# Feature-major weight tiles at all 64 pairs of eight start offsets

## The chip, the cores and the metric

The kernel runs on one core of a Trainium2 chip. The metric is the device time of one execution in microseconds. Engines are named as the profile does: PE is TensorE's matmuls, PEld its weight loads, DVE is VectorE, ACT is ScalarE, POOL is GpSimd, SP is SyncE, which issues most DMAs.

## The reference, cut to what matters

One encoder layer for 256 tokens of width 2048, all in float32. Nearly all of the arithmetic is seven dense products of an activation matrix with a weight matrix that is read once from HBM:

```python
proj = h @ w_in                              # 2048 x 18464, split into the heads of two mixers
x = x + merged @ w_out                       # 2048 x 2048
q = h @ w_q; k, v = split(mem_n @ w_kv)      # 2048 x 2048, 2048 x 4096
x = x + o @ w_o                              # 2048 x 2048
x = x + square(relu(h @ w_ff1)) @ w_ff2      # 2048 x 8192, 8192 x 2048
```

Between them lie norms, retention, a gated delta rule, and a cross-attention with four heads.

## The kernel before, in words

**Split operands.** Each float32 operand of a product is kept as a high part (`hi`, rounded to the type float32r by an ACT copy) and a low part (`lo`, the remainder, by a DVE subtraction). A product is then high x high + high x low + low x high. Activations stand in `Quad` tiles named `q`: four 128-row blocks of features, each with 256 high and 256 low columns beside each other.

**Weights.** `fetch` (L75) loads 1 MB of weights into a tile `raw` of [128, 2048] with one DMA on SP's queue, and splits it in two halves of 1024 columns: ACT writes `whi` (L93), DVE writes `wlo` (L94). Both names are rings of four buffers of 1024 + ROOM = 1088 columns, that is 4352 bytes in each partition, and ROOM lets the 1024 columns in use start a little after the buffer's start. `raw` is a ring of three. The fetches have the highest priority, so that they run ahead of the products as far as the rings allow.

**Two kinds of calls.** `chunk` (L120) is token-major: a block of activations is the stationary operand of TensorE, 512 columns of weights are the moving operand, and three matmuls (L134 to L136) make a product. `blocks` (L158) is feature-major: a block of 128 weight columns is stationary and the activations move. With `nb = 2`, which all calls use, one call takes 256 weight columns over all 16 blocks of 128 rows. For each such block (a *step* here) it does two matmuls with a high weight block against 512 columns (the activation's high and low parts at once, L172), and then two with a low weight block against 256 columns (the high part, L174). A call has 16 steps, 64 matmuls and two fetches, or four pairs of `whi` and `wlo`. There are 96 such calls in the program: for the attention's keys, queries and output, for the parts of the mixers that are wanted feature by feature, for the output projection, and for the first MLP matrix.

A third kind, `seven_products` (L1014), does part of the second MLP matrix with weight tiles `sh` and `sl` as moving operands of 256 columns.

**Where the tiles lie.** In the built program each `whi`, `wlo` and `q` buffer starts 224 bytes after a multiple of 256 in its partition. `chunk` uses offset 0 in the weight buffers, so that stationary and moving operands start equally far after a multiple of 256. `blocks` passes `at=SHIFT`, 48 elements or 192 bytes, for both parts. So its weights start 160 bytes after a multiple of 256, against 224 for the activations. `seven_products` shifts `sh` and `sl` by the same SHIFT; there the stationary operand is at 224 and the moving one at 160. All blocks within a tile are multiples of 512 bytes apart, so that these distances hold for every matmul of a call.

The instruction order is made at build time by a scheduler; semaphores follow from the tiles.

Of the kernel before, what the change touches and what calls it, by code (L numbers as in the profile page):

```python
# [11 lines left out]
F32R = mybir.dt.float32r  # L12
# [5 lines left out]
P = 128  # L18
# [15 lines left out]
SHIFT, ROOM = 48, 64  # L34
# [16 lines left out]
def trunk(ctx: ExitStack, tc: tile.TileContext, x, mem, positions, norm_mix_g, w_in, conv_w, gdn_a_log, gdn_dt_bias,  # L51
# [8 lines left out]
    wp = ctx.enter_context(tc.tile_pool(name="wpipe", bufs=3))  # L60
# [5 lines left out]
    def stream_ps():  # L66
        s0 = psp.tile([P, 512], F32, name="s0", tag="s0", bufs=2)
        s1 = psp.tile([P, 512], F32, name="s1", tag="s1", bufs=2)
        return s0, s1
# [2 lines left out]
        return psp.tile([P, 512], F32, name="b", tag="b", bufs=4)  # L72


    def fetch(pieces, k, n, rush=False, hold=None, at=0):  # L75

        raw = wp.tile([P, k * n], F32, name="raw", tag="raw", bufs=3)
        rv = raw.rearrange("p (k n) -> p k n", k=k)
        with tc.high_priority(offset=100000):
            for off, ap in pieces:  # L80
                src = ap.rearrange("(k p) n -> p k n", p=P)
                for ks in ((slice(0, k // 2), slice(k // 2, k)) if rush else (slice(0, k),)):
                    nc.sync.dma_start(rv[:, ks, off:off + ap.shape[1]], src[:, ks, :])
            got = []
            for i in range(2):
                if hold:
                    both = hold().both
                    hi, lo = (both[:, a:a + 2, :].rearrange("p a s -> p (a s)") for a in (0, 2))
                else:
                    hi, lo = (wp.tile([P, 1024 + ROOM], F32R, name=e, tag=e, bufs=4)[:, at:at + k * n // 2]  # L90
                              for e in ("whi", "wlo"))
                src = raw[:, i * k * n // 2:(i + 1) * k * n // 2]
                act.activation(hi, src, AF.Copy)  # L93
                vec.tensor_sub(lo, src, hi.bitcast(F32))  # L94
                got.append((hi.rearrange("p (k n) -> p k n", n=n), lo.rearrange("p (k n) -> p k n", n=n)))
        return got
# [23 lines left out]
    def chunk(quads, pieces_of, evac, before=None, hold=None, between=None):  # L120
# [4 lines left out]
        if hold:  # L125
            parts[1:] = [(1, 0, 256, ps[1][:, :256]), (1, 256, 512, bank()[:, :256])]
        held = {q: fetch(pieces_of(q), 4, 512, hold=hold) for q in ((2, 3) if hold else ())}

        def products(q, i, part, halves):
# [8 lines left out]
        for q in range(4):  # L138
            if q not in held:
                if before:  # L140
                    before(q)
                halves = fetch(pieces_of(q), 4, 512, rush=before is not None and q == 0)
                for i in range(4):
                    for part in parts:
                        products(q, i, part, halves)
                    if between and i % 2:
                        between()
# [10 lines left out]
    def blocks(quads, w, c0, nb, evac, whole=None, ahead=50000):  # L158

        k = 16 // nb
        ps = stream_ps()
        n = nb * P
        for g in range(KT // k):
            halves = fetch([(0, w[g * k * P:(g + 1) * k * P, c0:c0 + n])], k, n, at=SHIFT)
            for i in range(k):
                kk = g * k + i
                xh, xhl = quads[kk // 4][0][:, kk % 4, :], quads[kk // 4].both[:, kk % 4, :]
                wh, wl = (a[:, i % (k // 2), :] for a in halves[i // (k // 2)])  # L170
                for b in range(nb):
                    pe.matmul(ps[b], wh[:, b * P:(b + 1) * P], xhl, start=kk == 0, stop=False)  # L172
                for b in range(nb):
                    pe.matmul(ps[b][:, :S], wl[:, b * P:(b + 1) * P], xh, start=False, stop=kk == KT - 1)  # L174
        if whole:
            with tc.high_priority(offset=50000):
                o = whole()
                for b in range(nb):
                    act.activation(o[:, b, :], ps[b][:, S:], AF.Copy)
                    vec.tensor_add(o[:, b, :], o[:, b, :], ps[b][:, :S])  # L180
                evac(o)
            return
        for b in range(nb):
            with tc.high_priority(offset=ahead):
                o = sm.tile([P, S], F32, name="bo", tag="bo", bufs=2)
                act.activation(o, ps[b][:, S:], AF.Copy)  # L186
                vec.tensor_add(o, o, ps[b][:, :S])  # L187
                evac(b, o)
# [146 lines left out]
    for k2 in range(8):  # L335
# [10 lines left out]
        for f in range(2):  # L346
            k = 2 * k2 + f
# [171 lines left out]
    for b2 in range(8):  # L519
        ko = kv.tile([P, 2, S], F32, name="ko", tag="vo", bufs=2)  # L520

        def evac_k(b, ps):
            vec.tensor_mul(ko[:, b, :], ps, mrow)

        blocks(memq, w_xkv[0], b2 * 256, 2, evac_k)
        nc.sync.dma_start(kt_d[:, 2 * b2:2 * b2 + 2, :], ko)
        for h in ((0,), (2, 4), (6, 8), (10,), (12,), (14,), (), ())[b2]:
            decays(h)
        if 2 <= b2 < 6:
            ret_decays(2 * b2 - 4)  # L530
# [20 lines left out]
    for q in range(4):  # L551
        at = slice(32 * q, 32 * q + 32)
# [6 lines left out]
    def gdn_stream(grp):  # L559
# [4 lines left out]
        for pr in range(2):  # L564
# [5 lines left out]
            for part, c0, bofs in ((1, C_GQ, 0), (0, C_GK, 16), (2, C_GV, 32)):  # L570
                def evac(b, ps, part=part, bofs=bofs):
                    if part < 2:
                        conv_silu(bofs + h0 + b, ps, kq[:, b, part, :])
                    else:
                        vt = mx.tile([P, S], F32, name="vt", tag="vt", bufs=2)
                        conv_silu(bofs + h0 + b, ps, vt)
                        vts.append(vt)
                blocks(h1, w_in[0], c0 + h0 * GD, 2, evac)
# [171 lines left out]
    def retention(j, yr):  # L750
        qk = mx.tile([P, 4, S], F32, name="qk", tag="qk", bufs=1)

        for a2, c0 in ((0, C_RQ), (2, C_RK)):
            def evac_qk(b, ps):

                rb = mx.tile([P, S], F32, name="rb", tag="rb", bufs=2)
                act.activation(rb[0:64], ps[64:128], AF.Copy)
                act.activation(rb[64:128], ps[0:64], AF.Copy)
                o = qk[:, a2 + b, :]
                vec.tensor_mul(o, ps, cos)  # L760
                vec.tensor_mul(rb, rb, sin)
                vec.tensor_add(o, o, rb)

            blocks(h1, w_in[0], c0 + 256 * j, 2, evac_qk)
# [169 lines left out]
    for h in range(XH):  # L934
# [32 lines left out]
        for d2 in range(2):  # L967
            ops = bank()
            ov = ops.rearrange("p (d s) -> p d s", d=2)
            for d in range(2):  # L970
                c0 = (2 * d2 + d) * P
# [94 lines left out]
    for fb in range(4):  # L1066
# [6 lines left out]
        for b2 in range(8):  # L1073
# [3 lines left out]
            at = slice(b2 % 2 * 2, b2 % 2 * 2 + 2)  # L1077
# [15 lines left out]
        for n in range(1, 4):  # L1093
# [13 lines left out]
            def evac_last(t, ps, c0, c1):  # L1107
# [20 lines left out]
                for c in (0, 3, 1, 2):  # L1128
# [17 lines left out]
                  hold=quad_b if last else None)  # L1146
# [37 lines left out]
```

## Time and profile before

| | |
|---|---|
| time, median of 2 runs | 2065.16 us (2065.08 to 2065.25) |
| profiled execution | 2066.05 us, its span 2064.3 us |
| PE busy | 2045.1 us, 99% of the span |
| DVE busy | 1510.3 us, 73% |
| ACT busy | 1132.2 us, 55% |
| granted TensorE clock | 0.999 |
| HBM traffic | 197 GB/s over the span |

The span runs from the first to the last instruction; 1.75 us of the profiled execution lie outside it. A matmul's listed duration includes its passage through the array, in which the next one has already begun. The pace of matmuls is therefore read from the start of one to the start of the next, not from durations.

### The profile page before, as it was taken

Reading aid. Unit: us, or ns where it says so; the run is one execution under the profiler, and the core shown is the slowest. Engines: PE = TensorE matmul, PEld = TensorE weight load, DVE = VectorE, ACT = ScalarE, POOL = GpSimd, SP = SyncE. Lnnn points to the kernel's source line nnn. Section 1 sums busy time; section 2 is a strip of 40 time slices with the busy share of each in tenths; the row PEclk is TensorE's granted clock in tenths of the full one; section 3 lists DMA queues with packets and bytes.
Section 4 is the critical chain, followed back from the end, with each engine's and each line's share of the span. In section 5 each row is a group of like instructions: output and inputs, shape, how many; then the busy total and the mean of one; then the engine's idle time right before and its main releaser. Section 6 shows DMA issues by size and latency. Waiting matters only on the chain.

```text
span 2064.3 us, 29089 instructions
## 1 busy us (share of the span) xinstructions
PE 2045.1 (99%) x11240; PEld 1774.0 (86%) x11240; DVE 1510.3 (73%) x2381; ACT 1132.2 (55%) x1669; POOL 26.9 (1%) x37
## 2 busy tenths in 40 slices
PE   8999999999999999999999999999999999999998
PEld 6888888888888888888888898888888888988887
DVE  6785888588957896688767665768758756775885
ACT  7564664556445644565456555555546545554664
POOL 0000000000000000000000000000000000000000
PEclk9999999999999999999999999999999999999999
DMA  8797655465556555655567664565656566656653
GB/s 302 229 313 233 207 192 199 164 208 181 198 183 199 183 195 189 189 182 180 189 192 234 194 193 147 182 189 181 224 184 198 179 204 194 194 194 195 192 198 129
DMA packets 328313, 408.28 MB, mean 198 GB/s; under 512 B 31200, under 2 KB 236528, under 8 KB 328048
## 3 DMA queue, kind: packets, MB, share of 16 engines
q1 hardware_dynamic: 328032, 405.92, 61.0%
q8 instruction: 88, 1.44, 0.3%
q10 hardware_dynamic: 144, 0.52, 0.1%
q14 instruction: 49, 0.40, 0.1%
HBM read 391.19 MB, written 15.22 MB: 197 GB/s over the span
## 4 chain that ended last, share of the span: by engine, by line
PE 97%; DMA 1%; SPq 1%; issue 0%; DVE 0%; ACT 0%; POOLq 0%; POOL 0%; DVEq 0%; ACTq 0%
PE s L172 34%; PE s L174 17%; PE s L135 12%; PE s L134 12%; PE s L136 12%; PE b L1041 1%; PE b L1042 1%; PE b L1043 1%; PE b L689 1%; DMA xc<-x 1%; PE b L590 1%; PE b L104 0%; PE b L105 0%; PE b L106 0%; SPq L290 0%
## 5 line engine op out<-in xcount | busy, mean ns | idle before, releaser
L94 DVE TENSOR_TENSOR wlo<-raw,whi 128x1024 fp32r<-128x1024 f32 x668 | 816.0, 1223 | 412.6 <-ACT whi L93 405.7
L93 ACT ACTIVATE whi<-raw 128x1024 fp32r<-128x1024 f32 x668 | 706.6, 1060 | 689.1 <-PE s L172 331.2
L172 PE MATMUL s<-q,whi 128*128 128x512 f32 x3072 | 959.7, 392 | 2.2 <-DVE bo L187 2.1
L174 PEld LDWEIGHTS s<-q,wlo 128*128 128x128 f32 x3072 | 575.3, 188 | 123.6
L174 PE MATMUL s<-q,wlo 128*128 128x256 f32 x3072 | 611.9, 280 | 0.0
L172 PEld LDWEIGHTS s<-q,whi 128*128 128x128 f32 x3072 | 468.8, 188 | 5.2 <-DVE bo L187 2.5
L134 PE MATMUL s<-whi,q 128*128 128x512 f32 x1136 | 443.6, 392 | 0.7 <-ACT whi L93 0.7
L135 PE MATMUL s<-wlo,q 128*128 128x512 f32 x1136 | 443.5, 390 | 0.6 <-DVE wlo L94 0.6
L136 PE MATMUL s<-whi,q 128*128 128x512 f32 x1136 | 441.8, 390 | 0.0
L135 PEld LDWEIGHTS s<-wlo,q 128*128 128x128 f32 x1136 | 213.9, 188 | 43.5 <-DVE wlo L94 1.1
L134 PEld LDWEIGHTS s<-whi,q 128*128 128x128 f32 x1136 | 213.7, 188 | 42.9 <-ACT whi L93 1.1
L136 PEld LDWEIGHTS s<-whi,q 128*128 128x128 f32 x1136 | 213.3, 188 | 42.8 <-DVE q L257 0.2
L541 DVE SCALAR_TENSOR_TENSOR acc<-bo,cw,acc 128x255 f32<-128x255 f32 (+1 forms) x144 | 61.3, 479 | 3.3 <-ACT acc L538 3.0
L1029 ACT ACTIVATE sh<-raw 128x768 fp32r<-128x768 f32 x32 | 27.1, 847 | 49.1 <-DMA raw<-w_ff 32.5
L187 DVE TENSOR_TENSOR bo<-bo,s 128x256 f32<-128x256 f32 x128 | 47.9, 415 | 0.0
L649 DVE TENSOR_TENSOR pr<-lw,tw 32x31 f32<-32x31 f32 (+15 forms) x124 | 40.2, 324 | 8.7 <-DMA lw<-scr_l 7.1
L651 DVE TENSOR_TENSOR tw<-tw,pr 32x31 f32<-32x31 f32 (+15 forms) x124 | 40.5, 327 | 2.2
L186 ACT ACTIVATE bo<-s 128x256 f32<-128x256 f32 x128 | 41.0, 370 | 0.0
L1030 DVE TENSOR_TENSOR sl<-tt,sh 128x1024 fp32r<-128x1024 f32 x32 | 39.1, 1223 | 0.0
L1029 ACT ACTIVATE sh<-tt 128x1024 fp32r<-128x1024 f32 x32 | 33.6, 1051 | 8.4 <-DVE tt L1023 8.4
L1043 PE MATMUL b<-sh,cm 128*128 128x256 f32 x128 | 35.5, 279 | 0.0
L1042 PE MATMUL b<-sl,cm 128*128 128x256 f32 x128 | 35.5, 279 | 0.0
(359 smaller groups left out, 1575.5 us busy)
## 6 DMA issues: line engine op xcount, KB each, us to landing
raw<-w_in SPq DMA_DIRECT2D x143, 1024.0 KB, 5.1
raw<-w_ff SPq DMA_DIRECT2D x128, 1024.0 KB, 5.8
raw<-w_xkv SPq DMA_DIRECT2D x31, 1024.0 KB, 6.4
raw<-w_out SPq DMA_DIRECT2D x16, 1024.0 KB, 5.9
raw<-w_xq SPq DMA_DIRECT2D x16, 1024.0 KB, 5.4
raw<-w_xo SPq DMA_DIRECT2D x16, 1024.0 KB, 5.4
dec_d<-dec_w SPq DMA_DIRECT2D x8, 384.0 KB, 7.9
dec<-dec_d SPq DMA_DIRECT2D x8, 384.0 KB, 4.2
```

The costliest lines, as they stand in the source:

```text
L93: act.activation(hi, src, AF.Copy)
L94: vec.tensor_sub(lo, src, hi.bitcast(F32))
L134: pe.matmul(o, xh, wh, start=first, stop=False)
L135: pe.matmul(o, xh, wl, start=False, stop=False)
L136: pe.matmul(o, xl, wh, start=False, stop=last)
L172: pe.matmul(ps[b], wh[:, b * P:(b + 1) * P], xhl, start=kk == 0, stop=False)
L174: pe.matmul(ps[b][:, :S], wl[:, b * P:(b + 1) * P], xh, start=False, stop=kk == KT - 1)
L187: vec.tensor_add(o, o, ps[b][:, :S])
L541: vec.scalar_tensor_tensor(acc[:, d:], ps[:, :S - d], cw[:, j, blk:blk + 1], acc[:, d:], op0=ALU.mult, op1=ALU.add)
L1029: act.activation(sh[:, xs, :], src, AF.Copy)
L1042: pe.matmul(o, lhs[0], sl[:, x, :], start=False, stop=False)
L1043: pe.matmul(o, lhs[1], sh[:, x, :], start=False, stop=last and i == 1 and (m % 2 == 1 or m == 6))
```

## The change

The single offset of `fetch` becomes a pair, one for the high and one for the low tiles. Each call of `blocks` takes a running number `u` and uses the offsets 8 (u mod 8) for the high parts and 8 (u // 8 mod 8) for the low parts, in elements: 0, 8, ..., 56, or 0 to 224 bytes in steps of 32. After 64 calls the pairs start again; the 96 calls use every pair, and those with a low offset of 0, 8, 16 or 24 twice. `chunk` keeps offset 0, `seven_products` its SHIFT.

```diff
+    placed = []
+
-    def fetch(pieces, k, n, rush=False, hold=None, at=0):
+    def fetch(pieces, k, n, rush=False, hold=None, at=(0, 0)):
...
-                    hi, lo = (wp.tile([P, 1024 + ROOM], F32R, name=e, tag=e, bufs=4)[:, at:at + k * n // 2]
-                              for e in ("whi", "wlo"))
+                    hi, lo = (wp.tile([P, 1024 + ROOM], F32R, name=e, tag=e, bufs=4)[:, a:a + k * n // 2]
+                              for e, a in zip(("whi", "wlo"), at))
...
         k = 16 // nb
+        u = len(placed)
+        placed.append(u)
         ps = stream_ps()
         n = nb * P
         for g in range(KT // k):
-            halves = fetch([(0, w[g * k * P:(g + 1) * k * P, c0:c0 + n])], k, n, at=SHIFT)
+            halves = fetch([(0, w[g * k * P:(g + 1) * k * P, c0:c0 + n])], k, n, at=(8 * (u % 8), 8 * (u // 8 % 8)))
```

In the built programs the order of instructions on every engine, their waits' places, the buffers' addresses and the shapes are the same before and after. What differs is the start address within the buffer of what L93 and L94 write and what the weight loads of L172 and L174 read.

## The prediction

> **What bounds the kernel now.** First the page's busy times, its clock row and the chain that ended last.
>
> ```profile
> PE 2045.1 (99%) x11240; PEld 1774.0 (86%) x11240; DVE 1510.3 (73%) x2381; ACT 1132.2 (55%) x1669; POOL 26.9 (1%) x37
> PEclk9999999999999999999999999999999999999999
> PE 97%; DMA 1%; SPq 1%; issue 0%; DVE 0%; ACT 0%; POOLq 0%; POOL 0%; DVEq 0%; ACTq 0%
> PE s L172 34%; PE s L174 17%; PE s L135 12%; PE s L134 12%; PE s L136 12%; PE b L1041 1%; PE b L1042 1%; PE b L1043 1%; PE b L689 1%; DMA xc<-x 1%; PE b L590 1%; PE b L104 0%; PE b L105 0%; PE b L106 0%; SPq L290 0%
> ```
>
> TensorE makes 97% of the chain, at full granted clock. The two matmul lines of the feature-major calls alone, L172 and L174, are 34% and 17% of 2064.3 us, about 1053 us. Does TensorE ever wait for the tiles that the change moves? The table of its waits, whole, and the groups of the two lines that write those tiles answer it.
>
> ```profile
> PE b L246 <- DMA xc<-mem: 4.8, 1, 4.8
> PE b L232 <- DMA grow<-norm_mem_g: 2.5, 1, 2.5
> PE s L172 <- DVE bo L187: 2.1, 2, 1.1
> PE s L134 <- ACT whi L93: 0.7, 1, 0.7
> PE s L135 <- DVE wlo L94: 0.6, 1, 0.6
> L94 DVE TENSOR_TENSOR wlo<-raw,whi 128x1024 fp32r<-128x1024 f32 x668 | 816.0, 1223 | 412.6 <-ACT whi L93 405.7
> L93 ACT ACTIVATE whi<-raw 128x1024 fp32r<-128x1024 f32 x668 | 706.6, 1060 | 689.1 <-PE s L172 331.2
> ```
>
> TensorE waited 10.7 us in all, and 1.3 us of it for `whi` and `wlo`, both times in a token-major call. The other way round, ACT stood idle 331.2 us before L93 because the matmuls of L172 still held a buffer. The weights are ready early. So the time of a feature-major call is the pace of its matmuls, and that pace is read from starts in the timeline. Here is the end of a token-major call and the start of a feature-major one ("x2" merges two matmuls; columns are start, us, engine, line, output and inputs), and then where the same call ends.
>
> ```profile
> 1534.14 0.39 PE L134 MATMUL s<-whi,q 128*128 128x512 f32 x1
> 1534.37 0.39 PE L135 MATMUL s<-wlo,q 128*128 128x512 f32 x1
> 1534.60 0.39 PE L136 MATMUL s<-whi,q 128*128 128x512 f32 x1
> 1534.82 0.62 PE L172 MATMUL s<-q,whi 128*128 128x512 f32 x2
> 1535.28 0.39 PE L174 MATMUL s<-q,wlo 128*128 128x256 f32 x2
> 1535.51 0.62 PE L172 MATMUL s<-q,whi 128*128 128x512 f32 x2
> ...
> 1545.17 0.62 PE L172 MATMUL s<-q,whi 128*128 128x512 f32 x2
> 1545.62 0.40 PE L174 MATMUL s<-q,wlo 128*128 128x256 f32 x2
> 1545.86 0.62 PE L172 MATMUL s<-q,whi 128*128 128x512 f32 x2
> ```
>
> The call begins at 1534.82 and the next one at 1545.86: 11.04 us for 16 steps, **0.690 us a step**. 96 calls of 16 steps are 1536 steps (3072 matmuls of L172, two a step), and 1536 x 0.690 = 1060 us, which agrees with the chain's 1053. The token-major triple takes 1534.82 - 1534.14 = 0.68, or 226.7 ns for 512 columns.
>
> **The change part by part.** Nothing is added, removed or moved in order: the same instructions, shapes, DMAs and buffers, in the same places of every queue. Three things could still change.
>
> *The writes.* L93 and L94 write at offsets of 0 to 56 elements. The trace has two of the offsets, 0 in token-major calls and 48 in feature-major ones, mixed in one group:
>
> ```profile
> L94 DVE TENSOR_TENSOR wlo<-raw,whi x668: 1149/1226/1245, 6.1 to 2036.1; 128x1024 fp32r<-128x1024 f32 x167
> L93 ACT ACTIVATE whi<-raw x668: 1039/1061/1096, 5.0 to 2034.0; 128x1024 fp32r<-128x1024 f32 x167
> ```
>
> All 668 lie between 1149 and 1245 ns and between 1039 and 1096 ns (least, median, most), so these two offsets cost at most some per cent. I put the writes at nothing. The cover is the idle time above: L93 would have to become 689.1 / 668, about 1 us, longer each time before ACT had no idle time left ahead of it; DVE has 554 us of idle time in the span, 0.8 us for each L94.
>
> *The matmul pace as a function of the offset.* This is the whole question. A weight load and a matmul read at the same time, so their places in memory may matter:
>
> ```profile
> 1535.40 0.30 PEld L172 LDWEIGHTS s<-q,whi 128*128 128x128 f32 x2
> 1535.74 0.42 PEld L174 LDWEIGHTS s<-q,wlo 128*128 128x128 f32 x2
> ```
>
> The load at 1535.74, of 0.19 us, is the one of L174 and begins 0.23 us after the matmul at 1535.51, just as that line's second matmul begins: the load for the next matmul runs beside the current one. The Trainium skill, page "TensorE: Matmul & The Clock Gate", section "Step-by-step: what each phase is for", says that TensorE has two independent read ports and that such a load takes no read bandwidth from the running matmul. By that rule the offsets are free and the sum of this change is zero. The rows do not settle this, because 256-column matmuls are seen at more than one pace. Here is `seven_products` twice, first its slower and then its faster pace, and a stretch of a token-major call with 256 columns.
>
> ```profile
> 1416.58 0.28 PE L1041 MATMUL b<-sh,q 128*128 128x256 f32 x1
> ...
> 1419.06 0.63 PE L172 MATMUL s<-q,whi 128*128 128x512 f32 x2
> 1421.18 0.62 PE L172 MATMUL s<-q,whi 128*128 128x512 f32 x2
> ...
> 1424.65 0.28 PE L1042 MATMUL b<-sl,q 128*128 128x256 f32 x1
> 1426.58 0.39 PE L172 MATMUL s<-q,whi 128*128 128x512 f32 x1
> ...
> 2036.13 0.40 PE L134 MATMUL s<-whi,q 128*128 128x512 f32 x1
> 2036.83 0.28 PE L134 MATMUL s<-whi,q 128*128 128x256 f32 x1
> 2037.54 0.40 PE L134 MATMUL s<-whi,q 128*128 128x512 f32 x1
> ```
>
> From 1416.58 to 1419.06 stand 21 matmuls: 118.1 ns each. From 1424.65 to 1426.58 stand 17: 113.5 ns. Six from 2036.83 to 2037.54: 118.3 ns. The feature-major call that begins at 1419.06 does its first three steps by 1421.18 at **0.707 us**, against the usual 0.690. So the pace depends on something besides the columns, and the same offsets show two paces: a phase between loads and matmuls that a call enters with, besides the place. The three distances between stationary and moving start that the kernel has (0 in token-major calls; 64 bytes one way in feature-major calls and the other way in `seven_products`) all lie between 113.5 and 118.3 ns for 256 columns. With distance 0, a feature-major step put together from token-major rows would be 2 x 226.7 + 2 x 118.3 = 690.0 ns in the usual phase, the same as now, and 2 x 233.3 + 2 x 118.3 = 703 ns in the slow one (2036.13 to 2036.83 is 0.70 for three).
>
> So of the eight offsets, 0, 16 and 48 elements have a row near them and show no cost of their own in the usual phase. The other five (8, 24, 32, 40, 56) have no row. Both bounds for such a step: at best every matmul goes at the fastest paces seen, 2 x 226.7 + 2 x 113.5 = 680 ns, which is 10 ns less; at worst it goes at 707 ns, which is 17 ns more. Over all 1536 steps that is **-15 us to +26 us**. I take, for these offsets, the slow pace in one step of three, since the usual pace is what all three distances with a row show most of the time and is the nearest. About 0.6 of the operands fall on the five offsets (5 of 8 for the high parts, 56 of 96 calls for the low parts): 1536 x 0.6 x 17 ns / 3 = 5 us.
>
> *The lead of the weights.* A longer call would give ACT and DVE more time, a shorter one less. At the lower bound they still have the idle time above, so no wait comes late.
>
> **Sum.** Against the profiled execution: 2066.05 + 5 = 2071. The median before is 0.9 us below that execution, so **2070 us**.
>
> **The rivals.**
>
> 1. *Offsets don't matter* (and the two paces are phase alone). For it: all three distances with rows give the same 690 ns. Against it: nothing but the paces' spread. Time: 2065.
>
> 2. *Some pairs are better.* If the five offsets stall less often, the faster pace of 113.5 becomes usual. Time at the bound: 2065 - 15 = 2050. To be faster by over 2% (41.3 us, which is also about what this measurement can tell from no change), each of the 6144 matmuls would have to lose 6.7 ns on average, more than the 118.1 - 113.5 = 4.6 ns between the paces seen. That needs a pace that no row shows.
>
> 3. *Offsets at odd multiples of 32 bytes are dear: slower.* Every tile that TensorE now reads in these products starts at a multiple of 64 bytes from every other (224 and 160 after a multiple of 256). The change puts half of the high tiles and half of the low ones, 3072 matmuls, on starts that are 32 bytes off that raster. If the two reads hinder each other there and a load runs partly behind its neighbour, each such matmul is longer by a part of the load's 0.19 us. An eighth of it, 24 ns, gives 3072 x 24 = 74 us and 2139; the whole of it would be 584 us. The rival decides from 41.3 us / 3072 = 13.4 ns per affected matmul. For it: no row excludes it. Against it: the dearest matmul in the rows above takes 233 ns for 512 columns, some 7 ns over the usual.
>
> 4. *The change does not do what it says*: were the pairs not all used, or the buffers moved, the sum would differ. The built program has the 64 pairs and unmoved buffers, so this gets no chance of its own.
>
> **How the numbers follow.** Forecast (slightly slower, 2066 to 2092): 0.50. Rival 1 (2064 to 2066): 0.20. Rival 2 within its bound (2048 to 2064): 0.16, and beyond 2%: 0.03. Rival 3 over 2%: 0.11. The range reaches from rival 2's bound to the worst of the slow pace with a little of rival 3, **2048 to 2096**, and leaves out about 0.14. Faster by over 2%: 0.03; within 2%: 0.86; slower: 0.11.
>
> **What would show it.** The page should keep PE at 99% with the same counts, and the waits of TensorE for `whi` and `wlo` should stay near 1.3 us: that tests the writes and the lead. The 96 calls, read from start to start, should mostly take between 10.9 and 11.4 us (16 steps at 680 to 707 ns), with the call's length a function of its pair that repeats after 64 calls; the token-major triple should stay at 0.68 us. If calls of all pairs take 11.04, rival 1 is right. If calls with an odd u stand out by over half a microsecond, rival 3 is. The prediction is wrong if any pairs run far outside 680 to 707 ns a step, since all of it rests on paces that were seen at three distances only.

## The result, and the profile after

| | before | after |
|---|---|---|
| time, median of 2 runs | 2065.16 us | 2079.64 us (2079.45 to 2079.84) |
| ratio | | 1.007, 95% interval 1.0054 to 1.0087 |
| profiled execution / its span | 2066.05 / 2064.3 us | 2079.45 / 2077.7 us |

The change makes the kernel 14.5 us slower. That lies within the range, on the side that was forecast, but is three times the rise in the sum. In the changed kernel L93, L94, L172 and L174 have become L95, L96, L176 and L178, and the token-major L134 to L136 have become L136 to L138. The page's busy times, clock, chain, and the groups that matter:

```profile
PE 2060.4 (99%) x11240; PEld 1779.9 (86%) x11240; DVE 1509.8 (73%) x2381; ACT 1132.3 (54%) x1669; POOL 26.9 (1%) x37
PEclk9999999999999999999999999999999999999999
PE 98%; DMA 1%; issue 0%; ACT 0%; DVE 0%; SPq 0%; POOLq 0%; POOL 0%; ACTq 0%
L96 DVE TENSOR_TENSOR wlo<-raw,whi 128x1024 fp32r<-128x1024 f32 x668 | 815.4, 1222 | 425.7 <-ACT whi L95 422.6
L95 ACT ACTIVATE whi<-raw 128x1024 fp32r<-128x1024 f32 x668 | 706.9, 1060 | 701.0 <-PE s L176 351.0
```

The counts are the same and the granted clock is 0.999 in both. The writes take what they took (1222 and 1060 ns against 1223 and 1060). ACT waits even longer for the matmuls to give a buffer back, 351.0 us against 331.2. All waits of TensorE's matmuls:

```profile
PE b L250 <- DMA xc<-mem: 4.7, 1, 4.7
PE b L236 <- DMA grow<-norm_mem_g: 2.6, 1, 2.6
PE s L176 <- DVE bo L191: 1.5, 2, 1.1
```

None is for `whi` or `wlo`. (One weight load of L137 still waits 0.5 us for `wlo`.) Taking the time from each matmul's start to the next and adding it up by line, the two feature-major lines grew by 10.0 us (L172, now L176) and 4.4 us (L174, now L178); no other line changed by more than 0.6 us. So the whole loss is in the pace of the feature-major matmuls. The timeline shows it from call to call, each beginning at one of these rows (calls with the pairs (48, 56) and (56, 56) in elements, then after "..." the one with (16, 0), and the call after it):

```profile
1343.00 0.62 PE L176 MATMUL s<-q,whi 128*128 128x512 f32 x2
1354.39 0.62 PE L176 MATMUL s<-q,whi 128*128 128x512 f32 x2
1365.48 0.63 PE L176 MATMUL s<-q,whi 128*128 128x512 f32 x2
...
1392.20 0.63 PE L176 MATMUL s<-q,whi 128*128 128x512 f32 x2
1403.61 0.62 PE L176 MATMUL s<-q,whi 128*128 128x512 f32 x2
```

11.39, 11.09 and 11.41 us. In each kernel, 47 of the 96 calls run through without other work on TensorE between their steps: before, each of them took 11.04 us, and now they take 11.09 to 11.41. Below is the mean step in ns of every pair, worked out from the starts in the trace, over all steps that no other work breaks into; the instruction order, which is the built program's, tells which call has which pair. Each entry rests on one or two calls. Eight steps of 776 to 811 ns are left out: the same steps of the same calls last 774 to 807 ns in the kernel before, so their length is not the offsets' doing.

```
high \ low   0      8     16     24     32     40     48     56   elements
 0         696.7  703.4  699.4  699.2  699.9  699.9  694.7  700.4
 8         700.8  702.7  697.4  702.8  701.7  704.1  700.7  702.7
16         712.2  700.0  694.3  699.4  700.1  713.5  694.4  698.7
24         700.0  700.1  700.7  703.7  703.5  700.1  705.4  694.6
32         706.9  699.8  705.4  700.4  699.7  700.1  703.1  699.3
40         702.6  704.4  709.2  700.1  708.3  700.0  699.3  699.6
48         699.9  700.3  703.2  694.3  703.3  706.8  690.1  712.4
56         693.7  699.3  704.3  694.2  696.7  700.1  697.3  693.1
```

The best is (48, 48), the pair of the kernel before; the next, (56, 56), is at 693.1. The mean of all these steps is 700.9 ns against 690.7 before; 10.2 ns x 1536 steps = 15.7 us, which is the loss but for what the other lines give back and the steps left out. Most calls settle within a few steps and then repeat a short pattern of steps (their *pace*) until other work breaks in or they end. In the kernel before, the pattern is 687 and 693 ns in turn.

### The profile page after: what moved, and what is told of

It is laid out like the page before. It is cut to its first block, busy times and chain, and to the rows that moved or that the text cites. A ratio compares the mean times of both kernels' runs of the same rounds, so it can differ in the third digit from the quotient of the medians.

```text
span 2077.7 us, 29089 instructions
## 1 busy us (share of the span) xinstructions
PE 2060.4 (99%) x11240; PEld 1779.9 (86%) x11240; DVE 1509.8 (73%) x2381; ACT 1132.3 (54%) x1669; POOL 26.9 (1%) x37
## 4 chain that ended last, share of the span: by engine, by line
PE 98%; DMA 1%; issue 0%; ACT 0%; DVE 0%; SPq 0%; POOLq 0%; POOL 0%; ACTq 0%
PE s L176 34%; PE s L178 17%; PE s L136 13%; PE s L137 13%; PE s L138 12%; PE b L1045 1%; PE b L1047 1%; PE b L1046 1%; PE b L693 1%; PE b L594 1%; PE b L106 0%; PE b L107 0%; PE b L108 0%; DMA vr<-vv_d 0%; DMA xc<-mem 0%
## 5 line engine op out<-in xcount | busy, mean ns | idle before, releaser
L96 DVE TENSOR_TENSOR wlo<-raw,whi 128x1024 fp32r<-128x1024 f32 x668 | 815.4, 1222 | 425.7 <-ACT whi L95 422.6
L95 ACT ACTIVATE whi<-raw 128x1024 fp32r<-128x1024 f32 x668 | 706.9, 1060 | 701.0 <-PE s L176 351.0
L176 PE MATMUL s<-q,whi 128*128 128x512 f32 x3072 | 968.3, 395 | 1.6 <-DVE bo L191 1.5
L178 PEld LDWEIGHTS s<-q,wlo 128*128 128x128 f32 x3072 | 574.9, 188 | 132.7
L178 PE MATMUL s<-q,wlo 128*128 128x256 f32 x3072 | 615.9, 281 | 0.0
L176 PEld LDWEIGHTS s<-q,whi 128*128 128x128 f32 x3072 | 472.7, 188 | 4.7 <-DVE bo L191 2.0
L137 PE MATMUL s<-wlo,q 128*128 128x512 f32 x1136 | 443.4, 390 | 0.0
L136 PE MATMUL s<-whi,q 128*128 128x512 f32 x1136 | 443.2, 392 | 0.0
L138 PE MATMUL s<-whi,q 128*128 128x512 f32 x1136 | 441.8, 390 | 0.0
L137 PEld LDWEIGHTS s<-wlo,q 128*128 128x128 f32 x1136 | 213.9, 188 | 43.0 <-DVE wlo L96 0.5
L138 PEld LDWEIGHTS s<-whi,q 128*128 128x128 f32 x1136 | 213.5, 188 | 43.0
L136 PEld LDWEIGHTS s<-whi,q 128*128 128x128 f32 x1136 | 213.8, 188 | 42.2 <-ACT q L260 0.4
L1033 ACT ACTIVATE sh<-tt 128x1024 fp32r<-128x1024 f32 x32 | 33.7, 1052 | 10.2 <-DVE tt L1027 10.2
L1025 DVE TENSOR_TENSOR tt<-raw 128x1024 f32<-128x1024 f32 x16 | 19.6, 1224 | 22.5 <-DMA raw<-w_ff 22.5
```

Source lines behind the costliest of these rows:

```text
L136: pe.matmul(o, xh, wh, start=first, stop=False)
L137: pe.matmul(o, xh, wl, start=False, stop=False)
L138: pe.matmul(o, xl, wh, start=False, stop=last)
L1033: act.activation(sh[:, xs, :], src, AF.Copy)
```

## The experiments

**Does the place set the pace, or the change of place from call to call?** By the first idea (theory 1, the place theory) each pair has its own pace; by the second (theory 2) only the change costs. In the first two runs all 96 calls have one pair: one of the dearest, (16, 0), and then (0, 0).

```diff
-... k, n, at=(8 * (u % 8), 8 * (u // 8 % 8)))
+... k, n, at=(16, 0))        # and in the second run: at=(0, 0)
```

> All 96 feature-major calls with the one pair (16, 0), which in the swept kernel had steps of 713 ns in both of its calls. If the place sets the pace (theory 1): 713 - 690 = 23 ns a step over 1536 steps, 35 us over the kernel before, about 2100. If it is the change of offsets from call to call that costs (theory 2): one pair only, so about 2065.

Measured: 2096.48 us, 1.0151 of the kernel before (1.0136 to 1.0166), or 31 us over it where theory 1 expected 35. Two calls in a row in the timeline, beginning at

```profile
1403.73 0.63 PE L176 MATMUL s<-q,whi 128*128 128x512 f32 x2
1415.14 0.64 PE L176 MATMUL s<-q,whi 128*128 128x512 f32 x2
```

are 11.41 us apart, 713 ns a step, and the median step of every one of the 96 calls is 713. The place sets the pace; the change from call to call is not needed for it.

Could it be where ACT and DVE write the tiles, and not where TensorE reads them? In the 47 calls of this run without other work, 7 steps have no write to `whi` or `wlo` beside them. They average 713.3 ns, the other 745 steps 713.1. So the slow pace does not come from a write under way.

> All feature-major calls with the pair (0, 0). Theory 1: 697 ns a step as in the swept kernel, 7 x 1536 = 11 us over before, about 2076. Theory 2: 2065. My prediction's step put together from token-major rows (690 ns at distance 0): 2065 as well.

Measured: 2073.82 us, 1.0041 (1.0026 to 1.0055), or 9 us over before where theory 1 expected 11 and theory 2 nothing.

```profile
146.08 0.63 PE L176 MATMUL s<-q,whi 128*128 128x512 f32 x2
157.22 0.63 PE L176 MATMUL s<-q,whi 128*128 128x512 f32 x2
```

11.14 us, 696 ns a step, as for this pair in the swept kernel (696.7 in the table). So distance 0, at which the prediction had put a step together from token-major rows to 690 ns, is not free in a feature-major call.

**Is it the distance between the operands, or the absolute address?** The kernel before with all tiles 32 bytes lower, and then the kernel before with only the feature-major weights 256 bytes further (the rings get the room for it; `sh` and `sl` keep their size and their offset).

```diff
-    cp.tile([P, 56], F32, name="pad0")
+    cp.tile([P, 48], F32, name="pad0")
```

> The kernel before with every tile moved down by 32 bytes, all distances kept. If only the distance between the two operands counts: 2065, with 0.690 us a step. If the raster of absolute addresses counts (rival 3 in another form): a step changes by several ns in feature-major and token-major calls, several us at least.

```diff
-SHIFT, ROOM = 48, 64
+SHIFT, ROOM = 48, 128
...
-... k, n, at=SHIFT)
+... k, n, at=(SHIFT + 64, SHIFT + 64))
```

> The kernel before with the feature-major offset 64 elements (256 bytes) further, 112 for both parts, and rings that have room for it. If only the distance within 256 bytes counts: 0.690 us a step and 2065. If the full distance counts: another pace, as between pairs of the sweep, 5 to 35 us over.

Measured: 2064.78 us, ratio 0.9998 (0.9988 to 1.0007), and 2065.95 us, ratio 1.0004 (0.9995 to 1.0013). Both are the time of before. Neither a common shift by 32 bytes nor 256 bytes more between the operands moves the pace; the mean step of both runs is within 0.1 ns of before. So far as these two shifts of one pair can show it, what counts is the distance of the operands within 256 bytes, not the address.

**One part alone.**

```diff
-... at=(8 * (u % 8), 8 * (u // 8 % 8)))
+... at=(8 * (u % 8), SHIFT))        # and in the second run: at=(SHIFT, 8 * (u % 8))
```

> The high tiles' offsets alone are swept, the low ones stay at 48. If the two parts' costs add (the matmuls of L176 took 10.0 of the 13.4 us in the swept kernel): about +10 us, 2075. If the pair decides as a whole: the mean of the swept kernel's column of low offset 48 is 701 ns against 691, so 10 x 1536 = 15 us, about 2080, although only half of the change is made.

> The low tiles' offsets alone are swept, the high ones stay at 48. If costs add: little more than the 4.4 us that the matmuls of L178 took in the swept kernel, about 2070. If the pair decides as a whole: the swept kernel's row of high offset 48 means 701 ns a step against 691, about 15 us, 2080.

Measured: 2076.60 us (ratio 1.0056, 1.0041 to 1.0071) with the high tiles swept, which lies between the two expectations. The upper one was too high: its column mean of 701 ns held three of the long steps that are left out above. Without them the column of low offset 48 has a mean of 698.1, or 11 us over before, and this run's own mean step is 698.4. That fits the pair as a whole, but the 10 us of adding costs lie too near to be told from it. With the low tiles swept it was 2078.60 us (1.0066, 1.0050 to 1.0083), which is close to what a pair as a whole gives and far from the 4.4 us of adding costs. The two losses, 11.4 and 13.6 us against the runs of the kernel before made beside them, sum to 25 us, far more than the 14.5 of the full sweep. The parts do not add: moving either one off 48 loses most of what moving both does. The traces show it by line, too: with only the low tiles moved, the time from start to start grew by 8.5 us on the matmuls of the high tiles (L176) and by 5.2 us on those of the low ones (L178); with only the high tiles moved, by 6.5 and 4.0 us. A tile's place changes the pace of matmuls that do not use it, in the same step. The load of the next weights, which runs beside the current matmul, could do that; the runs do not separate it from other causes.

**Are odd multiples of 32 bytes dear?**

```diff
-... at=(8 * (u % 8), 8 * (u // 8 % 8)))
+... at=(56, 56))
```

> All feature-major calls with the pair (56, 56), an odd multiple of 32 bytes for both parts. Rival 3 (odd multiples are dear): over 2080. Place theory: 693 ns a step as that pair had in the swept kernel, 3 x 1536 = 5 us over before, about 2070.

Measured: 2075.05 us, 1.0049 (1.0034 to 1.0064), 10 us over before: less than rival 3 expected, and twice the 5 us of the place theory. The timeline tells why. Four rows, each the start of a call, in two stretches:

```profile
1400.46 0.62 PE L176 MATMUL s<-q,whi 128*128 128x512 f32 x2
1411.55 0.62 PE L176 MATMUL s<-q,whi 128*128 128x512 f32 x2
...
1552.12 0.64 PE L176 MATMUL s<-q,whi 128*128 128x512 f32 x2
1563.43 0.63 PE L176 MATMUL s<-q,whi 128*128 128x512 f32 x2
```

The same pair takes 11.09 us in one call and 11.31 in another: 693 and 707 ns a step. By the median of its steps, 28 of 96 calls run at 707 and 68 at 693 or 694. Calls that follow each other directly keep the pace, and a stretch of other matmuls between them can change it. So a place has more than one possible pace. That what runs before the call picks one of them fits these rows; no run varied that alone.

**How fine is it?** Both parts at the same offset, one element (4 bytes) further in each call.

```diff
-... at=(8 * (u % 8), 8 * (u // 8 % 8)))
+... at=(u % 64, u % 64))
```

> Both parts at the same offset, which goes from 0 to 63 elements, one element further in each call. If places count in pieces of 32 bytes: calls with offsets 8 m to 8 m + 7 all take the pace that the pair (8 m, 8 m) had in the swept kernel (697, 703, 694, 703, 700, 700, 690, 693 ns a step), about 2076. If the pace follows every element: paces between and beyond these, and perhaps one under 690 ns.

Measured: 2080.75 us, 1.0077 (1.0057 to 1.0097). The paces change from element to element: within the first 32 bytes, offsets 0 to 7, the calls' median steps run from 687 to 707 ns, and for seven of these eight offsets the second call is within 1 ns of the first. So places do not count in pieces of 32 bytes. In one of the two calls with an offset of 27 elements, two steps lie between

```profile
1928.14 0.66 PE L176 MATMUL s<-q,whi 128*128 128x512 f32 x2
1929.62 0.66 PE L176 MATMUL s<-q,whi 128*128 128x512 f32 x2
```

or 740 ns each, the dearest settled pace of all (the other call runs at 703). Of the neighbours, both calls at 26 run at 700, one call at 28 runs at 700, and the other takes 697 and 710 in turn. The cheapest is 7 elements with 687.

**A version that might win.** So all feature-major calls were put at (7, 7).

```diff
-... at=(8 * (u % 8), 8 * (u // 8 % 8)))
+... at=(7, 7))
```

> All feature-major calls with both parts at 7 elements, which in the fine sweep had steps of 687 ns in one undisturbed call and of 700 in part of another. If the place alone sets the pace: 687 against 690, 5 us under before, about 2060. If a call can also lock into the pair's second pace, as with (56, 56), and half of them do: (687 + 700) / 2, 3 us to 6 us over before, about 2070.

Measured: 2065.93 us, ratio 1.0006 (0.9997 to 1.0015): no change, and midway between the two expectations. Again there are two paces:

```profile
1335.40 0.63 PE L176 MATMUL s<-q,whi 128*128 128x512 f32 x2
1346.60 0.63 PE L176 MATMUL s<-q,whi 128*128 128x512 f32 x2
...
1395.40 0.62 PE L176 MATMUL s<-q,whi 128*128 128x512 f32 x2
1406.38 0.62 PE L176 MATMUL s<-q,whi 128*128 128x512 f32 x2
```

11.20 and 10.98 us, 700 and 686 ns a step. By their medians 68 calls ran at 687 and 28 dearer, 24 of them at 700 and 4 at 706, so the cheap pace had more than the expected half, and the mean step of 690.9 is that of before. No version beat the kernel before.

**And the token-major calls?** Their weights are the moving operand. With the feature-major calls back at (48, 48), they were swept; the kernel has enough such calls for 36 of the pairs.

```diff
+        u = len(placed)
+        placed.append(u)
         ps = stream_ps()
         parts = [(t, 0, 512, ps[t]) for t in range(NT)]
...
-                halves = fetch(pieces_of(q), 4, 512, rush=before is not None and q == 0)
+                halves = fetch(pieces_of(q), 4, 512, rush=before is not None and q == 0,
+                               at=(8 * (u % 8), 8 * (u // 8 % 8)))
```

> Feature-major calls back at (48, 48); instead the weights of the token-major calls, their moving operand, are swept over the 64 pairs. Place theory: the triple of 0.680 us changes with the pair by some per cent, the mean is above 0.680, and the time 3 to 15 us over before. If moving weights are insensitive to their place: 0.680 for all pairs and about 2065.

Measured: 2079.60 us, 1.0071 (1.0051 to 1.0091). In the call with the pair (40, 16), three triples stand between

```profile
1002.68 0.39 PE L138 MATMUL s<-whi,q 128*128 128x512 f32 x1
...
1004.77 0.39 PE L138 MATMUL s<-whi,q 128*128 128x512 f32 x1
```

or 0.697 us each. Over all undisturbed triples the mean is 0.696, and the lowest median of a pair is that of (0, 0), 0.680, the one of before; it rests on its one call, the first of the kernel. The mean step of the feature-major calls is 690.9 ns, as before, so the loss is the triples'. The moving operand's place matters as the stationary one's does.

## Why the prediction was right, point by point

The measured time lies in the range and on the side of the forecast, and for the reason given: the pace of the feature-major matmuls. The size of the rise was not right, 14.5 us where the sum had 5. That the sum rose at all was partly luck: for the offsets without a row it took the slow pace and not the fast one, which it had in its rows too, and gave no reason for that choice; and it did not know what decided the sign, that the pair of the kernel before is the best of the 64.

- *What bounds the kernel.* Right. TensorE is at 99% after as before, and the time is the pace of its matmuls.
- *The writes, at nothing.* Right: 1222 and 1060 ns, as before.
- *The lead of the weights.* Right: TensorE's matmuls waited for `whi` and `wlo` 1.3 us before and not at all after.
- *Offsets 0, 16 and 48 show no cost of their own.* Wrong. This step was read from token-major calls and `seven_products`, where the mix of widths, their order and the moving operand are others; which of these matters is not shown. In a feature-major call the pair (0, 0) is at 696 to 697 ns also when it is used throughout (2074 us), and (16, 0) at 713. The nine pairs made of 0, 16 and 48 alone average 698.3 ns in the table, 8 ns over (48, 48), and the other 55 average 701.3: the pairs that were put at nothing cost nearly as much as the rest.
- *The slow pace in one step of three, for six tenths of the operands: 5 us.* Mis-sized. The term comes to 3.4 ns a step; the mean rose by 10.2. Nearly all pairs cost something, since of the 64 only one is as low as 690. The term also counts the operands one by one, as if the high and the low tile each had a cost of its own; the runs with one part swept lost 11.4 and 13.6 us, which do not add up to the 14.5 of both.
- *The bounds of 680 and 707 ns a step.* They held for the mean, not for every pair: (16, 0) gives 713, 6 ns beyond, and 27 elements, outside the sweep, 740 in one call. The lower bound was never reached; 686 to 687 is the lowest settled pace.
- *Rival 1, offsets don't matter.* Refuted by the run with (16, 0), 31 us from the kernel before by the offset alone. The Trainium skill, page "TensorE: Matmul & The Clock Gate", section "Step-by-step: what each phase is for", says that a weight load takes no read bandwidth from the running matmul, which gave zero for this change. The trace does not agree with that zero: the same matmuls take 690 or 713 ns a step by the place alone, and the measurement decides. Whether the two reads share a port, no run here shows.
- *Rival 2, some pairs are better.* Of the 64 none is. At (7, 7) the calls have a better pace and a worse one, and come out even.
- *Rival 3, odd multiples of 32 bytes are dear.* Refuted: the pairs of the table with both offsets odd (8, 24, 40, 56) average 700.1 ns, those with both even 700.2, those with one of each 701.5.

What stays open is the mechanism itself. That loads and matmuls run beside each other is in the trace, and that the distance of their operands sets the pace is shown by the runs, for the places tried; that their reads collide in the memory is argued only, since no run took the loads away. What makes a call settle in one of two paces is open as well.

## What to carry to other kernels

Where back-to-back matmuls bound a kernel, read their pace from start to start, per call, and treat the distance between the stationary and the moving operand as a tuning parameter: here the step from the best pair tried to one of the dearest, (16, 0), was worth 1.5% with nothing else changed. Measure it in the loop that will use it, since the step put together from other loops' rows was wrong, and judge a place by a run in which all calls use it, because one call may show only one of its paces. A sweep that gives each call another offset is a cheap way to read many places from one profile; its own time is their mean, which was worse than a place already chosen well.

## What the runs showed of the hardware that was not expected

- The same matmuls on the same tiles settle in a repeating pattern of steps, and with (56, 56) and (7, 7) in one of several such patterns: 693 or 707 ns, and 687 or 700 ns and in parts of a few calls 707.
- The pace of a step depends on the distance to the element: 740 ns in a call at 27 elements, 700 at 26. It does not change over 256 bytes more (2065.95 us) or when all tiles move together (2064.78 us).
